# One mixer layer in float32: the down projection as Strassen's seven products, and another order of ScalarE's copies and norms

## The chip, the cores and the metric

The kernel runs on one core of one Trainium2 chip, as one launch. The metric is the device time of one execution in microseconds (us), the lower the better. A core has five instruction streams: TensorE (PE) multiplies matrices, VectorE (DVE) and ScalarE (ACT) work element by element, GpSimd (POOL) does small work and issues DMAs, SyncE (SP) issues DMAs only. They run side by side, each in its own order, and wait for each other by semaphores. Tiles live in SBUF (128 partitions), products are summed up in PSUM banks of 128x512 values, tensors named `..._d` lie in DRAM.

## The reference, cut to what matters

```python
def reference(x, c, ...):
    mod = silu(c) @ w_ada + b_ada
    sh1, sc1, g1, sh2, sc2, g2 = split(mod, 6)
    h = x * (1 + sc1) + sh1
    z = h @ w_in + b_in                        # seven slices of 256
    y = concat(short_conv(z), pool(z), conformer(z), ssm(z)) @ w_o
    x = layer_norm(ALPHA * x + (1 + g1) * y, ln1_g, ln1_b)
    h = x * (1 + sc2) + sh2
    f = (silu(h @ w_gate) * (h @ w_up)) @ w_down
    return layer_norm(ALPHA * x + (1 + g2) * f, ln2_g, ln2_b)
```

There are 1024 tokens, the model's width is 1024, the inner width of the last part (`D_FF`) is 2816 = 22 x 128, all in float32.

## The kernel before

Every float32 product is made of three matmuls of a short type: an operand is split into a high half (a cast on ACT, L80) and a low half (a subtraction on DVE, L81), and `passes` (L130 to L132) adds high x high, high x low and low x high into one PSUM bank. A pair of halves that waits for its matmuls is called a pair tile (`pr`); a wait on L80 or L81 is a wait for such a half.

The work comes in stages: input projection and mixers (0 to about 250 us), output projection and first layer norm of the first token half, gate and up projection with the mixers of the second half in between, the output projection and norm of the second half (about 390 to 515 us), then the rest of the gate and up projection by Strassen's scheme (515 to 785 us), then the down projection and the second norm. The code is written as generators. `in_order` keeps TensorE (and in places DVE and ACT) in the order in which the code is written; the other engines' instructions are put into order by a scheduler. `after(later, earlier)` orders two instructions of one engine without a wait.

**Mixers and output projection.** `out_prep(n, k)` makes the pair tile of 128 rows of `w_o` and the pair `ys` of one of the eight mixer outputs `y`; `out_step` multiplies them; `half(w3, c)` is the last slice of the input projection, which `short_out(1)` needs. `conformer(1)` ends with a norm: L457 scales on ACT, then transposes (L463) and a Silu (L464).

**Gate and up.** `c11(j)` makes the first two products of column block j for the first token half: after the first, `c11_mm` copies two banks on ACT (L643, "the copies of first products", tile `p1`), and only then TensorE goes on in the same banks. The norm of the second half (`ln1`, c = 1) is interleaved with it: its L580 scales a row tile on ACT, as soon as POOL has made the scale. `strassen(j)` makes the other five products of block j: inputs `a_ops(j)` (sums and differences of weight tiles, L725, and their pairs), products into banks `Z` and `X`, and after each product a DVE sum that reads the bank and lets TensorE go on (L757, L761, L767, L774, L778, two each). L769 and L781 multiply Silu(gate) by up, and POOL stores the products to `act_d` (L770, L782). The tiles `hi` come from a pool of three (`tmp`). `ada(j)` computes a column block of `mod` on DVE; `spread` writes a piece of `mod` to DRAM and reads it back as a row for all partitions (L470, tile `rowa_d`), and its last use, for g2, falls into Strassen's stage.

**Down.** For each token half c and each f of 22, `down_ops` loads `act_d` and `w_down`, makes both pairs, and `down_mm` multiplies them into eight banks (4 blocks t of 128 tokens, 2 halves h of the width): 2 x 22 x 4 x 2 x 3 = 1056 matmuls. `res2` and `ln2` then make the residual and the norm (L833, L834, statistics, a chain of small POOL steps for the inverse root, L841, L845), of the first token half beside the second's matmuls, and of the second as the tail.

## Time and profile before

| | |
|---|---|
| median of 3 executions | 1039.09 us (1038.07 to 1041.19) |
| the profiled execution, its time | 1037.87 us |
| its span, first to last instruction | 1036.1 us |
| TensorE busy | 980.8 us, 4480 matmuls |
| VectorE busy | 737.7 us |
| ScalarE busy | 344.5 us |
| GpSimd busy | 184.4 us |
| DMA | 177.75 MB, mean 172 GB/s |

Busy times are sums over the span of 1036.1 us; the time of an execution is 1.8 us longer than the span. The profile gives the granted clock of TensorE as a share of the full one, so 1.00 is 2.4 GHz and 0.50 is 1.2 GHz.

### The profile page before, as it was taken

To read this page: it belongs to the slowest core of one execution; us is meant where nothing else is said; L and a number is where in the kernel's file an instruction comes from. 1 tells how busy PE (TensorE), PEld (TensorE's weight loads), DVE (VectorE), ACT (ScalarE), POOL (GpSimd) and SP (SyncE) were. 2 spreads that over 40 slices of the span, in tenths; PEclk is the share of its full clock that TensorE was granted. 3 is DMA by queue.
4 is the path that set the end of the run, shared out by engine and by line. 5 is a ranking of instruction groups with operands and counts; after the bars stand their busy time and mean duration, and the time that the engine had idled before them with its cause. 6 is when DMAs were issued, how large, how long until landed. Compare 5 with 4: busy or idle time off the path is not lost.

```text
span 1036.1 us, 12527 instructions
## 1 busy us (share of the span) xinstructions
PE 980.8 (95%) x4480; PEld 799.9 (77%) x4480; DVE 737.7 (71%) x1184; ACT 344.5 (33%) x537; POOL 184.4 (18%) x515
## 2 busy tenths in 40 slices
...
GB/s 314 321 112 104 53 41 90 219 225 223 158 204 172 147 237 104 188 316 267 347 175 159 138 147 152 146 148 111 82 149 284 174 136 142 232 185 148 228 21 61
DMA packets 65694, 177.75 MB, mean 172 GB/s; under 512 B 11040, under 2 KB 17216, under 8 KB 65632
## 3 DMA queue, kind: packets, MB, share of 16 engines
...
## 4 chain that ended last, share of the span: by engine, by line
PE 60%; DVE 10%; DMA 5%; POOL 4%; ACT 3%; issue 2%; SPq 0%; DVEq 0%; POOLq 0%; ACTq 0%
PE mm L132 18%; PE mm L130 18%; PE mm L131 17%; PE sm L130 2%; PE sm L132 2%; PE sm L131 2%; DMA raw<-in_w_ada_dram 2%; DMA raw<-h_d 2%; DVE pr L81 1%; DVE acc L429 1%; DMA raw<-in_w_gate_dram 1%; DVE raw L168 1%; ACT tmp L598 1%; DVE lst L500 1%; POOL rs_a L397 1%
## 5 line engine op out<-in xcount | busy, mean ns | idle before, releaser
L81 DVE TENSOR_TENSOR pr<-raw,pr 128x1024 fp32r<-128x1024 f32 (+1 forms) x139 | 138.1, 1003 | 77.7 <-ACT pr L80 77.4
L80 ACT CAST pr<-raw 128x1024 fp32r<-128x1024 f32 (+1 forms) x139 | 119.2, 878 | 179.4 <-PE sm L132 68.4
L130 PE MATMUL mm<-bop,pr 128*128 128x512 f32 x264 | 103.2, 391 | 4.2 <-DVE c L767 3.5
L131 PE MATMUL mm<-bop,pr 128*128 128x512 f32 x264 | 102.8, 389 | 0.0
L132 PE MATMUL mm<-bop,pr 128*128 128x512 f32 x264 | 102.7, 389 | 0.0
L130 PE MATMUL mm<-h,pr 128*128 128x512 f32 (+1 forms) x208 | 77.0, 370 | 8.0 <-ACT p L643 7.1
L429 DVE SCALAR_TENSOR_TENSOR acc<-up,pack,acc 128x512 f32<-128x512 f32 x120 | 84.3, 742 | 0.1
L130 PE MATMUL mm<-pr,acts 128*128 128x512 f32 x216 | 84.0, 389 | 0.0
L131 PE MATMUL mm<-pr,acts 128*128 128x512 f32 x216 | 84.0, 389 | 0.0
L132 PE MATMUL mm<-pr,acts 128*128 128x512 f32 x216 | 84.0, 389 | 0.0
L132 PE MATMUL mm<-h,pr 128*128 128x512 f32 (+1 forms) x208 | 75.4, 362 | 2.9 <-DVE pr L81 2.9
L131 PE MATMUL mm<-h,pr 128*128 128x512 f32 (+1 forms) x208 | 75.2, 361 | 0.0
L132 PE MATMUL mm<-tb,pr 128*128 128x512 f32 x176 | 68.8, 391 | 1.1 <-DVE pr L81 1.0
L130 PE MATMUL mm<-tb,pr 128*128 128x512 f32 x176 | 68.7, 390 | 1.0 <-ACT pr L80 1.0
L131 PE MATMUL mm<-tb,pr 128*128 128x512 f32 x176 | 68.5, 389 | 0.0
L397 POOL TENSOR_SCALAR rs_a<-lmv 128x1 f32<-128x1 f32 x16 | 11.0, 689 | 318.1 <-DVE lmv L503 317.8
L168 DVE SCALAR_TENSOR_TENSOR raw<-raw,cond 128x1024 f32<-128x1024 f32 x48 | 58.1, 1218 | 13.3 <-DMA raw<-in_w_ada_dram 13.2
L80 ACT CAST pr<-room 128x512 fp32r<-128x512 f32 x60 | 34.3, 619 | 87.9 <-PE mm L132 83.9
L130 PEld LDWEIGHTS mm<-bop,pr 128*128 128x128 f32 x264 | 49.6, 188 | 16.4 <-DVE c L767 2.9
L132 PEld LDWEIGHTS mm<-bop,pr 128*128 128x128 f32 x264 | 49.6, 188 | 10.3
L131 PEld LDWEIGHTS mm<-bop,pr 128*128 128x128 f32 x264 | 49.6, 188 | 10.1
L131 PE MATMUL mm<-h_a,pr 128*128 128x512 f32 x104 | 42.7, 410 | 13.7 <-DVE h_a L81 13.5
...
## 6 DMA issues: line engine op xcount, KB each, us to landing
...
```

The lines of the kernel that those rows point to most:

```text
L80: S.copy(hi, src)
L81: V.tensor_tensor(out=lo, in0=src, in1=hi.bitcast(F32), op=SUB)
L130: PE.matmul(o, wh, xh, start=first, stop=False, skip_group_check=True)
L131: PE.matmul(o, wh, xl, start=False, stop=False, skip_group_check=True)
L132: PE.matmul(o, wl, xh, start=False, stop=last, skip_group_check=True)
L168: V.scalar_tensor_tensor(out=w, in0=w, scalar=1.0, in1=cond, op0=MUL, op1=MUL, accum_out=mod[:, j:j + 1])
L397: G.tensor_scalar(out=a, in0=v, scalar1=EPS, scalar2=None, op0=ADD)
L429: V.scalar_tensor_tensor(out=o, in0=u, scalar=dww[:, i, j:j + 1], in1=o, op0=MUL, op1=ADD)
L500: V.bn_stats(st[:, h], r[:, h * 512:(h + 1) * 512])
L598: S.activation(dst, src, AF.Identity, scale=hA[:, kk:kk + 1], bias=hB[:, kk:kk + 1])
```

## The change

The down projection is taken as a product of 2 x 2 blocks (token halves and inner halves on one side, inner halves and width halves on the other) and made of seven block products instead of eight, each over 11 blocks j: 7 x 11 x 4 x 3 = 924 matmuls. The sums of activations that five of the products need are made in `strassen(j)` as soon as the activations are there (L794 to L798, four of 128x512 on DVE) and stored to a new tensor `s_d` (two stores of 512 KB on POOL's queue, L797 and L799); for that the product of the first token half is read back from `act_d` (L777, 256 KB), and the store that stood in that place is gone. The product of the second token half's gate and up stays in SBUF until the sums are made. The differences of weights are made on DVE beside the products (`t13`, `t2`, `t34`). One product after another is summed up in four banks (`oA`) or the other four (`oB`); results that are wanted later are copied out by ACT. There are seven pair tiles where there were four, `GR` groups two j for one load, and in the last product the four last groups run t by t.

In Strassen's loop the inputs of block j + 1 (`a_ops`) are now begun ahead of the sums of block j. Before 515 us: both halves of `w3` are multiplied ahead of `out_prep`; `ada(32)` and `ada(33)` come later; the second part of `conformer(1)` is placed one c11 block later; the norm activations of `conformer(1)` and of `ln1` for c = 1 are ordered behind the latest copy of a first product; the order of `ln1` and `c11` around the output projection of the second half differs.

```diff
@@ -454,8 +454,10 @@
         G.tensor_scalar(out=nb, in0=nb, scalar1=-1.0, scalar2=None, op0=MUL)
         yield
         for t in range(4):
-            S.activation(nt[:, t * 256:(t + 1) * 256], tp[t // 2][:, (t % 2) * 256:(t % 2) * 256 + 256],
-                         AF.Identity, scale=rs[:, t:t + 1], bias=nb[:, t:t + 1])
+            i = S.activation(nt[:, t * 256:(t + 1) * 256], tp[t // 2][:, (t % 2) * 256:(t % 2) * 256 + 256],
+                             AF.Identity, scale=rs[:, t:t + 1], bias=nb[:, t:t + 1])
+            if c == 1 and t == 0:
+                after(i, copied[-1])
...
@@ -577,7 +580,9 @@
         nb = cst.tile([P, 1], F32, name="lnb", bufs=2)
         G.tensor_scalar(out=nb, in0=nm, scalar1=rs, scalar2=-1.0, op0=MUL, op1=MUL)
         yield
-        S.activation(r, r, AF.Identity, scale=rs, bias=nb)
+        i = S.activation(r, r, AF.Identity, scale=rs, bias=nb)
+        if c == 1:
+            after(i, copied[-1])
...
+    copied = []
+
     def c11_mm(w, z, p1, q, lo=0, n=CH):
 
         hs = slice(lo, lo + n)
         for i in range(2):
             product(z[i][:, hs], w[i], q, ("11", "21")[q], q == 0, q == 1, hs)
             if q == 0:
-                S.copy(p1[:, i * CH + lo:i * CH + lo + n], z[i][:, hs])
+                copied.append(S.copy(p1[:, i * CH + lo:i * CH + lo + n], z[i][:, hs]))
...
-    def strassen(j):
-
-
-        ao = a_ops(j)
-        w = next(ao)
+    def strassen(j, ao=None, w=None):
+
+
+        ao = ao or a_ops(j)
+        w = w or next(ao)
...
@@ -767,7 +774,7 @@
             V.tensor_tensor(out=c12[m], in0=c12[m], in1=X[m], op=ADD)
         S.activation(c12[0], c12[0], AF.Silu)
         V.tensor_tensor(out=c12[0], in0=c12[0], in1=c12[1], op=MUL)
-        G.dma_start(act_d[2 * j][:, CH:], c12[0])
+        G.dma_start(c12[1], act_d[2 * j][:, :CH])
...
-    def down_ops(c, n):
-        b0, b1 = FB[c][n]
-        w, act = {}, {}
-        more = sl.tile([P, 4, 2, 1024], F32R, name="wd", tag="ha") if b1 - b0 > 3 or c == 1 and n == 0 else None
-        if c == 1 and n == 0:
-            dn["first"] = more
-        for f in range(b0, b1):
-            a = raw_p.tile([P, 1024], F32, name="raw", tag="raw", bufs=4)
-            SP.dma_start(a[:, :CH], act_d[f][:, cs(c)])
-            act[f] = acts[(c * FT + f) % 8]
-            split(act[f][:, 0], act[f][:, 1], a[:, :CH])
-            if c == 1 and n < 4:
-                w[f] = dn["first"][:, n]
-            elif f < b1 - 3:
-                w[f] = more[:, f - b0]
-            else:
-                w[f] = pair_tile()
-            split(w[f][:, 0], w[f][:, 1], raw(A["w_down"][f]))
-        dn[c][n] = w, act
...
+        yield
+
+        a11, a21, (a12, a22) = c12[1], c12[0], [hi[0][:, H[c]] for c in range(2)]
+        (s1, s3), (s2, s4) = P1, [hi[1][:, H[c]] for c in range(2)]
+        V.tensor_tensor(out=s1, in0=a21, in1=a22, op=ADD)
+        V.tensor_tensor(out=s2, in0=s1, in1=a11, op=SUB)
+        V.tensor_tensor(out=s3, in0=a11, in1=a21, op=SUB)
+        G.dma_start(s_d[j, 0].rearrange("p a t -> p (a t)"), p1)
+        V.tensor_tensor(out=s4, in0=a12, in1=s2, op=SUB)
+        G.dma_start(s_d[j, 1].rearrange("p a t -> p (a t)"), hi[1])
+
+
+
+    GR = tuple((j, min(j + 2, FT // 2)) for j in range(0, FT // 2, 2))
...
+    def dn_pair(src, pt=None):
+        pt = pair_tile() if pt is None else pt
+        n = src.shape[1]
+        split(pt[:, 0, :n], pt[:, 1, :n], src)
+        return pt
+
+    def dn_mm(o, lt, rt, g, t, first, last):
+        n = GR[g][1] - GR[g][0]
+        for j in range(n):
+            ls, rs = slice(j * CH + t * P, j * CH + (t + 1) * P), slice(j * CH, (j + 1) * CH)
+            passes(o[t], (lt[:, 0, ls], lt[:, 1, ls]), (rt[:, 0, rs], rt[:, 1, rs]),
+                   first and g == 0 and j == 0, last and g == len(GR) - 1 and j == n - 1)
+
+    def dn_product(o, left, right, first, last, also=lambda g: None, room=(None, None)):
+        for g in range(len(GR)):
+            lt, rt = [dn_pair(x(g), None if g else y) for x, y in zip((left, right), room)]
+            for t in range(4):
+                dn_mm(o, lt, rt, g, t, first, last)
+            also(g)
...
@@ -884,11 +910,12 @@
         zz.append(half(w2, 1))
         short_out(0, zz)
         fin1()
+        zz = [half(w3, c) for c in (1, 0)][::-1]
         for n in range(2):
             wy.append(out_prep(n, K0[n]))
-            ada(32 + n)
         acc, taps = conv(1)
-        zz = [half(w3, c) for c in range(NCH)]
+        for j in range(32, 34):
+            ada(j)
         g1row = spread(mod[:, 16:24], "rowa")
         for j in range(34, 40):
             ada(j)
@@ -977,7 +1004,9 @@
                 run(taps)
                 conf = conformer(1, acc, sm)
                 with tc.high_priority():
-                    run(conf, 2)
+                    run(conf, 1)
+            if f == CF + 1:
+                run(conf, 1)
...
@@ -1004,11 +1033,13 @@
             cc.extend(c11(j) for j in range(GU_FIRST + 2, FT // 2))
             run(cc[0], 1)
         out_proj1(mid, done)
+        run(ln[0], 1)
         for t in range(4):
-            run(ln[t], 1)
             if t % 2 == 0:
                 run(cc[t // 2 + 1], 1)
             run(cc[t // 2], 1)
+            if t < 3:
+                run(ln[t + 1], 1)
             run(ln[t])
...
-        run(st)
+        run(st, 2)
         room = sl.tile([P, 8, 1024], F32, name="room", tag="ha")
         for j in range(1, FT // 2):
-            run(strassen(j))
+            ao = a_ops(j)
+            w = next(ao)
+            run(st)
+            st = strassen(j, ao, w)
+            run(st, 5)
             if j > 1 and j < 10:
                 ada(38 + j)
+        run(st)
...
+    pairs.extend((sl, f"m_{n}", 1) for n in ("up", "zch", "zp"))
     with in_order(ON_PE):
-        last = len(FB[0]) - 1
...
+        r0, r1 = [[yp.tile([P, 1024], F32, name="r2", tag=f"y{4 * c + t}") for t in range(4)] for c in range(2)]
+        oA = [mm() for _ in range(4)]
+        oB = [mm(), mm(), sm(), sm()]
...
+        def t13(g):
+            b12, b11, b22 = (w_rows(g, b, h, tmp()) for b, h in ((0, 1), (0, 0), (1, 1)))
+            V.tensor_tensor(out=kept(g), in0=b12, in1=b11, op=SUB)
+            V.tensor_tensor(out=kept(g, True), in0=b22, in1=b12, op=SUB)
+
+        def t2(g):
+            b22, o = w_rows(g, 1, 1), kept(g)
+            V.tensor_tensor(out=o, in0=b22, in1=o, op=SUB)
+            return o
+
+        def t34(g):
+            b21, o = w_rows(g, 1, 0), kept(g)
+            V.tensor_tensor(out=o, in0=b21, in1=o, op=SUB)
+            return kept(g, True)
+        dn_product(oA, lambda g: act_rows(g, 0, 0), lambda g: w_rows(g, 0, 0), True, False, t13)
         for t in range(4):
-            run(res2(o0, t, rr[t], x1[t]))
-        for n in range(len(FB[1])):
-            if n > 3:
-                down_ops(1, n)
...
+            S.copy(r0[t][:, H[0]], oA[t])
+        ln0, ln1_ = [[ln2(c, t, (r0, r1)[c][t]) for t in range(4)] for c in range(2)]
+        dn_product(oB, lambda g: sum_rows(g, 0, 0), kept, True, False)
+        x1 = [keep_x1(0, t, kx[:, t] if t < 3 else tmp()) for t in range(4)]
+        for t in range(4):
+            res2(r0[t], x1[t], 0, r0[t][:, H[0]])
+        dn_product(oA, lambda g: sum_rows(g, 1, 0), t2, False, False)
+        for t in range(4):
+            S.copy(r0[t][:, H[1]], oA[t])
+        dn_product(oA, lambda g: sum_rows(g, 0, 1), t34, False, False)
+        for t in range(4):
+            res2(r0[t], x1[t], 1, r0[t][:, H[1]])
+        x1 = [keep_x1(1, t, kx[:, t] if t < 3 else tmp()) for t in range(4)]
+        for t in range(4):
+            S.copy(r1[t][:, H[1]], oA[t])
+            V.tensor_tensor(out=r1[t][:, H[1]], in0=r1[t][:, H[1]], in1=oB[t], op=ADD)
+        dn_product(oA, lambda g: act_rows(g, 1, 1), kept, False, True)
+        for t in range(4):
+            res2(r1[t], x1[t], 1, r1[t][:, H[1]])
+            run(ln1_[t], 1)
+        for t in range(4):
+            res2(r1[t], x1[t], 0, oA[t])
+
+        more0 = sl.tile([P, 2, 2, 1024], F32R, name="wd0", tag="hb0")
+
+        def more_res(t, h, o):
+            f = sl.tile([P, CH], F32, name="f", tag=f"acc{t % 2}")
+            V.tensor_tensor(out=f, in0=o, in1=g2row[:, H[h]], op=MUL)
+            V.tensor_tensor(out=r0[t][:, H[h]], in0=r0[t][:, H[h]], in1=f, op=ADD)
+        dn_product(oA, lambda g: act_rows(g, 1, 0), lambda g: w_rows(g, 1, 0), True, True,
+                   room=[more0[:, i] for i in range(2)])
+        for t in range(2):
+            run(ln1_[t])
+        more = sl.tile([P, 4, 2, 1024], F32R, name="wd", tag="ha")
...
+        ops = []
+        for g in range(len(GR)):
+            two = (None, None) if g < len(GR) - 2 else [more[:, 2 * (g - len(GR)) + 4 + i] for i in range(2)]
+            ops.append((dn_pair(sum_rows(g, 1, 1), two[0]), dn_pair(w_rows(g, 1, 1), two[1])))
+            if g < last:
+                for t in range(4):
+                    dn_mm(oB, *ops[g], g, t, False, True)
+            if g in (1, 3):
+                run(ln1_[2 + g // 2])
+        for t in range(4):
+            more_res(t, 0, oA[t])
+            run(ln0[t], 1)
+        for t in range(4):
+            for g in range(last, len(GR)):
+                dn_mm(oB, *ops[g], g, t, False, True)
     with in_order(ON_DVE):
         for t in range(4):
-            run(ln[t], 2)
-            if t == 2:
-                run(ln[3], 1)
-            run(ln[t])
+            more_res(t, 1, oB[t])
+            run(ln0[t], 1)
+            if t:
+                run(ln0[t - 1])
+            run(ln0[t], 1)
+        run(ln0[3])
```

Three places show what the change moves. The first is ACT at about 233 us of the kernel before, in the first steps of the output projection. `ys` are the pairs of mixer outputs, `pr_2149` (before) and `pr_2150` (after) is the pair tile of the third `w_o` block. Before:

```order
L852 ACTIVATE y0_1164<-mm_1938,pack0_88 128x512
L381 ACTIVATE y3_1167<-mm_1968,pack2_471 128x512
L80 CAST pr_2149<-raw_2147 128x1024
L80 CAST ys_1976<-y4_1168 128x512
L80 CAST ys_1976<-y5_1169 128x512
L80 CAST ys_1976<-y2_1166 128x512
L80 CAST ys_1976<-y3_1167 128x512
L852 ACTIVATE y1_1165<-mm_2021,pack0_88 128x512
L80 CAST ys_1976<-y0_1164 128x512
```

After:

```order
L878 ACTIVATE y0_1164<-mm_1939,pack0_88 128x512
L381 ACTIVATE y3_1167<-mm_1969,pack2_471 128x512
L80 CAST ys_2027<-y4_1168 128x512
L80 CAST ys_2027<-y5_1169 128x512
L80 CAST ys_2027<-y2_1166 128x512
L80 CAST ys_2027<-y3_1167 128x512
L878 ACTIVATE y1_1165<-mm_1972,pack0_88 128x512
L80 CAST ys_2027<-y0_1164 128x512
L80 CAST pr_2150<-raw_2148 128x1024
```

The pair tile's cast stood ahead of the four `ys` casts and now comes behind all of them.

The second is ACT at about 429 us of the kernel before, in the norm of the second token half. `r1` is a row tile of that norm, `p1` the copy of a first product. Before:

```order
L580 ACTIVATE r1_3530<-r1_3530,lnb_3552,lrs_3536 128x1024
L80 CAST pr_3349<-raw_3670 128x1024
L80 CAST pr_3674<-raw_3675 128x1024
L580 ACTIVATE r1_3568<-r1_3568,lnb_3590,lrs_3574 128x1024
L643 COPY p1_3681<-mm_3679 128x512
L643 COPY p1_3681<-mm_3680 128x512
L598 ACTIVATE tmp_3718<-mm_3708,hB_1647,hA_1646 128x128 x4
```

After:

```order
L583 ACTIVATE r1_3531<-r1_3531,lnb_3553,lrs_3537 128x1024
L80 CAST pr_3350<-raw_3671 128x1024
L80 CAST pr_3675<-raw_3676 128x1024
L650 COPY p1_3682<-mm_3680 128x512
L650 COPY p1_3682<-mm_3681 128x512
L583 ACTIVATE r1_3569<-r1_3569,lnb_3591,lrs_3575 128x1024
L603 ACTIVATE tmp_3721<-mm_3711,hB_1647,hA_1646 128x128 x4
```

The two copies stood behind the second norm activation and now stand ahead of it.

The third is DVE at the boundary of two blocks in Strassen's loop (a middle one). `tmp_4915`, `tmp_4916` (before) and `tmp_4940`, `tmp_4941` (after) are the `hi` tiles of block j, the next two `tmp` those of block j + 1; `room_4331` and `room_4332` hold weights and first products. Before:

```order
L781 TENSOR_TENSOR tmp_4915<-tmp_4915,tmp_4916 128x1024
L81 TENSOR_TENSOR pr_5163<-room_4331,pr_5163 128x512
L757 TENSOR_TENSOR tmp_5102<-room_4331,mm_5104 128x512
L757 TENSOR_TENSOR tmp_5103<-room_4331,mm_5105 128x512
L81 TENSOR_TENSOR pr_5168<-room_4331,pr_5168 128x512 x2
L761 TENSOR_TENSOR c12_5100<-room_4331,mm_5104 128x512
```

After:

```order
L788 TENSOR_TENSOR tmp_4940<-tmp_4940,tmp_4941 128x1024
L796 TENSOR_TENSOR room_4332<-c12_4938 128x512
L794 TENSOR_TENSOR room_4332<-c12_4938,tmp_4940 128x512
L764 TENSOR_TENSOR tmp_5133<-room_4332,mm_5135 128x512
L795 TENSOR_TENSOR tmp_4941<-room_4332,c12_4938 128x512
L81 TENSOR_TENSOR pr_5194<-room_4332,pr_5194 128x512
L798 TENSOR_TENSOR tmp_4941<-tmp_4940,tmp_4941 128x512
L81 TENSOR_TENSOR pr_5199<-room_4332,pr_5199 128x512
L764 TENSOR_TENSOR tmp_5134<-room_4332,mm_5136 128x512
```

Between the product of the two activations (L781, now L788) and the second sum that frees a bank (the second L757, now L764) stood two instructions, and now seven do, four of them the new sums. In the pool of three, `tmp_5134` gets the buffer of `tmp_4940`, so the second L764 waits for the store of `tmp_4940` to `act_d`, which was not so before.

## Rows read from the trace of the kernel before

**Rows 1.** The page: busy us, share of the span, instructions, by engine.
```profile
PE 980.8 (95%) x4480; PEld 799.9 (77%) x4480; DVE 737.7 (71%) x1184; ACT 344.5 (33%) x537; POOL 184.4 (18%) x515
```
**Rows 2.** TensorE's waits: whom for, us in total, times, longest us.
```profile
PE mm L130 <- ACT p L643: 7.1, 2, 4.2
PE mm L132 <- DVE pr L81: 3.9, 4, 2.0
...
PE mm L130 <- ACT ys L80: 2.9, 1, 2.9
...
PE mm L132 <- DVE ys L81: 1.3, 1, 1.3
```
**Rows 3.** Stretches: us, busy by engine (instructions), granted clock, DMA share, GB/s.
```profile
237.70:244.50 6.80, 6.04 (x14) 4.79 (x15) 6.80 (x15) 1.35 (x3) 0.00 (x0) 0.50 0.67 232
...
432.20:439.10 6.90, 5.81 (x14) 4.56 (x15) 1.58 (x3) 5.22 (x14) 4.82 (x14) 0.51 0.53 210
...
515.00:785.00 270.00, 268.96 (x1186) 222.16 (x1185) 202.98 (x323) 75.66 (x121) 10.25 (x19) 1.00 0.42 147
...
785.10:1024.60 239.50, 239.50 (x1057) 198.05 (x1055) 141.25 (x171) 64.86 (x81) 27.26 (x64) 1.00 0.46 161
```
**Rows 4.** Timeline: start us, us, engine, instruction, [idle before, releaser]; loads and ACT, 231 to 238.
```profile
231.53 0.33 SPq L73 DMA_DIRECT2D raw<-in_w_o_dram  x1
...
234.83 1.04 ACT L80 CAST pr<-raw 128x1024 fp32r<-128x1024 f32 x1 [11.49 <-DMA raw<-in_w_o_dram]
235.78 2.17 ACT L80 CAST ys<-y 128x512 fp32r<-128x512 f32 x4
```
**Rows 5.** Timeline of ACT, 369 us.
```profile
369.34 1.93 ACT L457 ACTIVATE tmp<-sm,cnb,crs 128x256 f32<-128x256 f32 x4 [5.19 <-POOL cnb L454]
```
**Rows 6.** Timeline of ACT, 431 to 434 us.
```profile
431.53 1.24 ACT L580 ACTIVATE r<-r,lnb,lrs 128x1024 f32<-128x1024 f32 x1 [5.41 <-POOL lnb L578]
432.67 1.05 ACT L643 COPY p<-mm 128x512 f32<-128x512 f32 x2
```
**Rows 7.** Timeline of DVE and POOL at a boundary of two blocks, 620 to 629 us.
```profile
620.53 0.69 DVE L778 TENSOR_TENSOR tmp<-room,mm 128x512 f32<-128x512 f32 x1 [2.03 <-PE mm L132]
621.23 0.69 DVE L81 TENSOR_TENSOR pr<-room,pr 128x512 fp32r<-128x512 f32 x1
621.83 1.22 DVE L781 TENSOR_TENSOR tmp<-tmp 128x1024 f32<-128x1024 f32 x1
622.97 0.69 DVE L81 TENSOR_TENSOR pr<-room,pr 128x512 fp32r<-128x512 f32 x1
...
625.97 0.69 DVE L757 TENSOR_TENSOR tmp<-room,mm 128x512 f32<-128x512 f32 x1 [1.72 <-PE mm L132]
...
628.69 0.69 DVE L761 TENSOR_TENSOR c<-room,mm 128x512 f32<-128x512 f32 x1 [0.72 <-PE mm L132]
...
623.35 0.54 POOL L782 DMA_DIRECT2D act_d<-tmp  x1 [10.74 <-DVE tmp L781]
```
**Rows 8.** Landing of L782's stores and of L470's writes; timeline, 705 to 720 us.
```profile
DMA to landing us min/median/max: 2.9/2.9/8.6
...
L470 SPq DMA_DIRECT2D rowa_d<-mod x2: 377/378/378, 202.6 to 699.6; - x2
...
DMA to landing us min/median/max: 9.5/10.3/11.1
...
705.19 0.54 POOL L782 DMA_DIRECT2D act_d<-tmp  x1 [10.86 <-DVE tmp L781]
...
719.69 0.47 PE L130 MATMUL mm<-bop,pr 128*128 128x512 f32 x1 [1.04 <-DVE c L767]
```
**Rows 9.** Groups by line, 785 to 1025 us (busy us, mean ns); timeline of the tail.
```profile
L81 DVE TENSOR_TENSOR pr<-raw,pr 128x1024 fp32r<-128x1024 f32 x33 | 40.3, 1220 | 51.9 <-ACT pr L80 51.8
...
1025.17 0.68 DVE L833 TENSOR_TENSOR r<-sm,row 128x512 f32<-128x512 f32 x1
```

93 lines of the change are left out of this document (44 added, 49 removed).

## The prediction

> **What bounds the kernel now.** I read the page's engine shares first [rows 1]: TensorE (PE) is busy 95% of the span and VectorE (DVE) 71%, and the large stages run at the full clock [rows 3]. So TensorE is the bound, and there are two ways to gain: fewer matmuls, or fewer of the idle stretches that make up the other 5%. The waits of TensorE [rows 2] name what ends those stretches; the table of stretches [rows 3] tells which stages have none. The down stage, 785.1 to 1024.6 us, is one block: 1057 matmuls in 239.50 us, 0.2266 us each from start to start. Strassen's stage before it (515 to 785) is busy 268.96 of 270 us. The idle time therefore lies before 515 us, and in the 11.5 us between 1024.6 and the end. Two idle stretches are followed by stretches at a granted clock of about half, which is the 1.2 GHz level: 6.8 us after the wait at 233 to 236, and 6.9 us after the wait at 429 to 433. Each such stretch does half its length of full-speed work, so it costs about 3.4 us beyond the wait itself.
>
> **Down projection, matmuls.** Before: 2 token halves x 22 f x 4 t x 2 h x 3 passes = 1056. After: 7 products x 11 j x 4 t x 3 = 924. The 132 that go are of the shape whose pace is in [rows 3]: 132 x 0.2266 = 29.9 us less, if the stage stays without gaps. This is the one sure term.
>
> **Down projection, its operands.** Per group of two j (24 matmuls, 5.4 us) DVE makes the low halves of two 128x1024 pairs: at 1.22 us each [rows 9], 2.4 us. The weight differences add two such subtractions in the groups of product 1 and one in those of products 3 and 4, so product 1 needs 4.9 of each 5.4 us, if it is made at that pace; in the order its differences trail into product 2, which needs them later. With the residuals, the norms and the two rows scaled, I count 188 us of DVE work behind the last Strassen sum, against some 221 us of stage and tail; before it was 141 us in 239.5 [rows 3]. DVE becomes a close second. It is tightest in products 6 and 7: the instructions from the residual of product 5's result to the last pair come to 46 us, and the last pair is wanted about 45 us after that result. The copies of first products out of PSUM and the four-bank hand-overs between products add short chains of one ACT or DVE instruction (0.6 to 0.7 us each); the second bank set is free at most of them. Bounds: 0, if the pair tiles run ahead all the way, and 8 us, if every hand-over (six) shows a copy of 0.7 us and DVE is 4 us late at the end. I take 2 us.
>
> **Sums inside Strassen's loop.** Each of 11 rounds (27.2 us) gets four 128x512 DVE sums (0.60 us apiece start to start, 2.4 us) and two 512 KB stores, and loads 256 KB instead of storing it. DVE has room in the mean: 202.98 of 270 us busy [rows 3], plus 10 x 2.4. The place that matters is the boundary of two rounds, in the third piece of order. Let B be the end of a round's last product, 620.5 us in [rows 7], where L778 stops waiting for TensorE. Before, the second L757 began at 625.97 and ended its idle wait on TensorE: DVE was early. After, the product of the two activations is followed by seven 128x512 instructions before the second L764: 621.83 + 1.14 + 7 x 0.6 = 627.2 us, done at 627.9 (1.14 and 0.60 are the steps from one start to the next in these rows). TensorE overwrites that bank when its next product ends, and L761 began on that at 628.69; so about 0.6 us of margin is left. L764 also waits for something new: its tile is the one that the store of L789 reads. That store, like L782 before, is issued at 623.35 and lands 2.9 us later [rows 7, 8], at 626.3, in time too. The loads of the next round's gate and up tiles follow it and now share the DMA engines with two 512 KB stores. I bound the ten boundaries by 0 (margin holds) and 10 us (1 us each, about the margin again), and take 2 us.
>
> **One bad boundary.** At 699.6 us the spread of g2 (L470, writes of 4 KB in all to rowa_d) is issued; the two such spreads took 9.5 and 11.1 us to land [rows 8]. The store of L782 that is issued in that time, at 705.19, I take for the one that landed after 8.6 us, where the median of the eleven is 2.9. Before, only loads waited for it, and TensorE lost 1.04 us at 719.69. After, the second L764 of the next round waits for this store: 705.19 + 8.6 = 713.8, plus 0.7 for itself, while TensorE wants the bank at B + 8 = 710.3. That is a wait of about 4 us, perhaps followed by 3.4 us of clock as at 429 us, and the old 1.0 us goes. Bounds 0 and 7; I take +4 us. The Trainium skill, "DMA: Bandwidth & Descriptors", section "Queues, rings and completion order", says that a DMA's semaphore increment lands only after every earlier write of the same DMA engine, across its queues. By that rule the late landing comes again, and the term stays at +4; if it was chance, the term would be -1. The 8.6 us beside 2.9 agrees with the rule.
>
> **Order changes before 515 us.** At 234.83 us ScalarE (ACT) cast a w_o pair whose load had only been issued at 231.53, and the four ys casts behind it kept TensorE waiting 2.9 us, and their low halves on DVE another 1.3, with half clock behind [rows 2 to 4]. After, these casts come before that pair (first piece of order): 4.2 us of waits and 3.4 of clock go. Next late are the w_o pairs of the following steps, made at DVE's and the loads' pace; I give back 1.6 and take -6 us, bounds -3 and -7.6. At 369 us the copies of a first product (L643) stood behind four norm activations that had waited 5.19 us for POOL [rows 5]: 2.9 of the 7.1 us in [rows 2], which go; the activations are the later part of a norm whose transposes follow only in the output projection. I take -3, bounds -3 and 0. At 431.53 us the same copies stood behind a norm activation (L580) that waited for POOL [rows 6]: 4.2 us of wait and 3.4 of clock. After, the copies come first (second piece). The norms, the tb pairs and the stores behind them start no earlier than before while TensorE arrives 7 us sooner, so part may come back up to 515: I take -6, bounds -2 and -7.6. At 288 us one w_up pair was 2.0 us late on DVE [rows 2]; it moves ahead in DVE's order. I take -1, bounds -2 and 0.
>
> **Tail.** The last four groups run t by t, 21 matmuls = 4.76 us per t, where DVE needs about 5.1 us per t; before there were 42. The chain after the last matmul is the same length: residual 0.7 us, 0.7 us, statistics, the POOL chain, two scalings and the store, 1025.17 to the end [rows 9]. I take +0.7, bounds 0 and 3.
>
> **Sum** against the profiled execution of 1037.87 us (span 1036.1): -29.9 + 2 (operands) + 2 (boundaries) + 4 (spread) - 6 (233 us) - 3 (368 us) - 6 (429 us) - 1 (288 us) + 0.7 (tail) = -37.2, so 1000.7. The median of the executions timed is 1.2 us above the profiled one, which gives **1002 us**.
>
> **Rivals.** *The early gaps only move.* The 16 us of gains before 515 us are worth nothing if the next pair, load or norm is late by the same: DVE is busy all of the 6.80 us around 240 [rows 3], which speaks for it; that the casts and copies had their data and stood only behind others' waits speaks against it. Keeping a fifth, 3 us: 1002 + 13 = 1015 us. *Nothing is lost late.* The margins hold, the down stage is gapless and the spread is absorbed: without the +8.7 and with the early gains at 18 instead of 16: 1002 - 11 = 991 us. Against it: the margins are under 1 us. *Every boundary becomes a DMA wait.* The store that L764 waits for lands late not once but in every round, since two more 512 KB stores and the prefetched gate and up loads of the next round lie around it. At the 8.6 us of [rows 8] a boundary costs 4 us and then 3.4 of half clock, 7.4 us; ten instead of one cost 67 us more: 1069 us, slower than before. It decides from six boundaries: the 37 us of the sum are eaten by five more than the one counted. For it: the landing time under load is shown once. Against it: the other stores of this kind have a median of 2.9 us, and the DMA engines are busy 42% in this stage, at 147 GB/s [rows 3]. *The change does not do what it says*: 924 matmuls stand in the order, so only the ScalarE part could fail, which is the first rival.
>
> **How the numbers follow.** Forecast (995 to 1009) 0.58; early gaps only move 0.20; nothing lost late 0.16; every boundary 0.04; something between, near no change, 0.02. The range from 990 to 1016 holds the forecast, the middle of its two neighbours, and leaves out under 2 in 10. A measurement of this kernel tells 0.3% (3 us) from no change. Faster by more: 0.95; within: 0.02; slower: 0.03.
>
> **What would show it.** In the changed profile: 924 matmuls in the last stage at 0.227 us, so about 210 us of it, and its waits on DVE pairs under 8 us; no wait on ACT ys near 233 and on p near 368 and 429, and no stretch at half clock behind them; one wait of TensorE of about 4 us near 690, behind an L764 that waits for a DMA; L764's waits elsewhere below 1 us; the tail about 12 us. The forecast is wrong if DVE is busy over 95% in products 6 and 7 with TensorE waiting for pairs, or if L764 waits in every round.

## The result, and the profile after

The changed kernel takes 1025.18 us (median of 4 runs, 1023.93 to 1026.33), beside 1040.09 us for the kernel before on the same chip (1038.07 to 1041.19): a ratio of 0.986, 95% interval 0.9836 to 0.9884. It is faster by 15 us (1.4%), but the forecast was 1002 us and the range ended at 1016. The profiled execution took 1024.31 us with a span of 1022.5, 13.6 us less than the span of before.

The page of after, busy us by engine, answers to [rows 1]; under it the stretches of after (us, busy by engine with instructions, granted clock, DMA share, GB/s), which answer to [rows 3]:

```profile
PE 960.3 (94%) x4348; PEld 779.2 (76%) x4348; DVE 807.9 (79%) x1268; ACT 358.0 (35%) x545; POOL 200.1 (20%) x537
```

```profile
0.00:225.00 225.00, 203.71 (x972) 158.68 (x973) 176.83 (x360) 74.18 (x114) 79.07 (x281) 0.95 0.51 160
225.00:515.00 290.00, 272.37 (x1267) 224.50 (x1266) 209.25 (x323) 129.98 (x222) 64.91 (x141) 0.96 0.62 214
515.00:791.70 276.70, 272.69 (x1189) 223.44 (x1189) 225.21 (x361) 75.25 (x119) 21.47 (x40) 0.99 0.54 186
791.70:1008.20 216.50, 211.49 (x925) 172.58 (x923) 187.99 (x216) 78.60 (x91) 26.43 (x58) 1.00 0.65 217
```

The 132 matmuls are gone (4480 to 4348). But the last line begins at 791.7 us, where the down stage of before began at 785.1: the kernel reaches that stage 6.5 us later, not 10 us earlier as the sum had it. And the mean clock of 225 to 515 us is lower than before. The same stretch of the kernel before:

```profile
225.00:515.00 290.00, 268.08 (x1266) 220.89 (x1265) 209.22 (x320) 129.70 (x222) 65.05 (x142) 0.98 0.60 215
```

TensorE's waits in after (whom for, us in total, times, longest), to be set beside [rows 2]:

```profile
PE mm L130 <- ACT p L650: 5.6, 2, 2.9
PE mm L131 <- DVE pr L81: 4.7, 5, 2.2
PE mm L132 <- DVE pr L81: 3.6, 4, 2.0
PE mm L130 <- DVE y L877: 3.2, 1, 3.2
PE mm L130 <- DVE tmp L764: 2.9, 2, 2.2
...
PE sm L130 <- ACT y L466: 2.0, 1, 2.0
```

The wait on ACT `ys` has fallen from 2.9 to 0.3 us; a wait on `y` from L877 stands there that was not, the one on L466 has grown from 0.5 to 2.0 us, and the copies of first products still cost 5.6 us where they cost 7.1.

Here is where the time went, measured on TensorE from the first matmul of each stage (profiled executions, us; "again" is a second profile of the changed kernel, from another session, "undone" is the kernel with all early order changes taken back, from the same session as "again"; the last three are kernels of the experiments, "best" the one with two edits):

| stage | before | after | after, again | undone | after, fewer loads | undone, fewer loads | best |
|---|---|---|---|---|---|---|---|
| start to first output step | 236.4 | 234.2 | 234.6 | 239.3 | 234.7 | 238.2 | 232.7 |
| to the second half's output projection | 140.9 | 141.2 | 141.4 | 140.5 | 139.3 | 140.5 | 137.0 |
| to Strassen's block 0 | 88.6 | 94.8 | 95.0 | 88.4 | 93.0 | 88.4 | 86.7 |
| blocks 0 and 1 | 72.7 | 73.8 | 74.7 | 77.4 | 68.3 | 68.4 | 78.5 |
| blocks 2 to 10 | 246.3 | 247.4 | 252.0 | 252.4 | 249.6 | 251.1 | 250.9 |
| down stage | 239.5 | 216.5 | 219.2 | 219.5 | 217.5 | 220.2 | 218.9 |
| tail | 11.5 | 14.5 | 14.5 | 14.4 | 14.5 | 14.5 | 14.5 |

Each column is one execution; "again" shows the slowest of its six (1033.12 us, median 1028.71). How far executions of one early order differ is shown by four kernels further down (the stores on POOL's queue, the spread moved, the reuse in product 1, three groups at the end), which have the same instructions in the same order as after up to 512 us on TensorE, VectorE, ScalarE and GpSimd. With the two of after that makes six profiles: they reach the first output step at 234.2 to 235.9 us, take 91.2 to 95.0 us in the third row, and begin block 2 (the first four rows together) at 541.3 to 545.9 us. The two profiles with the early order undone and full loads begin it at 545.4 and 545.7 us.

### The profile page after: what moved, and what is told of

The parts are those of the page before. It is cut to its first block, busy times and chain, and to the rows that moved or that the text cites. A ratio compares the mean times of both kernels' runs of the same rounds, so it can differ in the third digit from the quotient of the medians.

```text
span 1022.5 us, 12397 instructions
## 1 busy us (share of the span) xinstructions
PE 960.3 (94%) x4348; PEld 779.2 (76%) x4348; DVE 807.9 (79%) x1268; ACT 358.0 (35%) x545; POOL 200.1 (20%) x537
## 4 chain that ended last, share of the span: by engine, by line
PE 29%; issue 26%; DVE 11%; POOL 8%; DMA 7%; ACT 3%; SPq 0%; POOLq 0%; DVEq 0%; ACTq 0%
PE mm L132 9%; PE mm L130 9%; PE mm L131 9%; DVE pr L81 3%; DMA tmp<-in_w_down_dram 2%; DVE acc L429 1%; DMA raw<-in_w_ada_dram 1%; DVE raw L168 1%; POOL rs_b L402 1%; ACT tmp L603 1%; POOL rs_a L397 1%; DMA raw<-h_d 1%; ACT pr L80 1%; PE sm L130 1%; DMA raw<-in_w_o_dram 1%
## 5 line engine op out<-in xcount | busy, mean ns | idle before, releaser
L80 ACT CAST pr<-raw 128x1024 fp32r<-128x1024 f32 (+1 forms) x157 | 133.6, 876 | 178.5 <-PE mm L132 67.8
L81 DVE TENSOR_TENSOR pr<-raw,pr 128x1024 fp32r<-128x1024 f32 (+1 forms) x157 | 155.3, 1002 | 32.9 <-ACT pr L80 32.4
L131 PE MATMUL mm<-pr 128*128 128x512 f32 x250 | 97.9, 391 | 4.7 <-DVE pr L81 4.7
L130 PE MATMUL mm<-pr 128*128 128x512 f32 x250 | 97.4, 390 | 0.1
L132 PE MATMUL mm<-pr 128*128 128x512 f32 x250 | 97.3, 389 | 0.0
L429 DVE SCALAR_TENSOR_TENSOR acc<-up,pack,acc 128x512 f32<-128x512 f32 x120 | 84.6, 749 | 0.1
L130 PE MATMUL mm<-h,pr 128*128 128x512 f32 (+1 forms) x208 | 78.2, 376 | 6.5 <-ACT p L650 5.6
L132 PE MATMUL mm<-h,pr 128*128 128x512 f32 (+1 forms) x208 | 76.4, 367 | 2.9 <-DVE pr L81 2.9
L131 PE MATMUL mm<-h,pr 128*128 128x512 f32 (+1 forms) x208 | 76.6, 368 | 0.0
L130 PE MATMUL mm<-tb,pr 128*128 128x512 f32 x176 | 69.5, 395 | 2.9 <-DVE tmp L764 2.9
L132 PE MATMUL mm<-tb,pr 128*128 128x512 f32 x176 | 69.6, 396 | 0.7 <-DVE pr L81 0.7
L131 PE MATMUL mm<-tb,pr 128*128 128x512 f32 x176 | 69.0, 392 | 0.0
L131 PEld LDWEIGHTS mm<-pr 128*128 128x128 f32 x250 | 46.9, 188 | 16.2 <-DVE pr L81 6.7
```

Source lines behind the costliest of these rows:

```text
L80: S.copy(hi, src)
L81: V.tensor_tensor(out=lo, in0=src, in1=hi.bitcast(F32), op=SUB)
L130: PE.matmul(o, wh, xh, start=first, stop=False, skip_group_check=True)
L131: PE.matmul(o, wh, xl, start=False, stop=False, skip_group_check=True)
L132: PE.matmul(o, wl, xh, start=False, stop=last, skip_group_check=True)
L429: V.scalar_tensor_tensor(out=o, in0=u, scalar=dww[:, i, j:j + 1], in1=o, op0=MUL, op1=ADD)
```

## Where the early gains went

**At 238 us.** The `ys` come in time, and TensorE then stops 4 us later. DVE in after, 237 to 242 us, and TensorE (start us, us, engine, instruction, [idle before, releaser]):

```profile
238.08 1.21 DVE L168 SCALAR_TENSOR_TENSOR raw<-raw,cond 128x1024 f32<-128x1024 f32 x1
...
239.30 0.74 DVE L429 SCALAR_TENSOR_TENSOR acc<-up,pack,acc 128x512 f32<-128x512 f32 x1
...
240.69 0.74 DVE L877 SCALAR_TENSOR_TENSOR y<-mm,pack,y 128x512 f32<-128x512 f32 x1
```
```profile
237.90 0.39 PE L132 MATMUL mm<-pr,ys 128*128 128x512 f32 x1
241.49 0.50 PE L130 MATMUL mm<-pr,ys 128*128 128x512 f32 x1 [3.20 <-DVE y L877]
```

L877 reads the PSUM bank of one `w3` half. That half is now multiplied ahead of the output steps, so its bank is held until DVE, which has `ada` and the convolution (L429) in front, comes to it. The change took away a wait on casts and put a bank that is given back late in its place: 3.2 us for 4.2.

**At 446 and 463 us.** ACT in after, the copies of first products (L650), and TensorE behind them:

```profile
440.20 2.94 ACT L603 ACTIVATE tmp<-mm,hB,hA 128x128 f32<-128x128 f32 x8
...
444.07 2.08 ACT L80 CAST pr<-raw 128x1024 fp32r<-128x1024 f32 x2
445.96 1.16 ACT L650 COPY p<-mm 128x512 f32<-128x512 f32 x2
...
458.52 2.90 ACT L603 ACTIVATE tmp<-mm,hB,hA 128x128 f32<-128x128 f32 x8
...
462.39 1.12 ACT L650 COPY p<-mm 128x512 f32<-128x512 f32 x2
```
```profile
446.68 0.76 PE L130 MATMUL mm<-h,pr 128*128 128x512 f32 x1 [2.88 <-ACT p L650]
...
463.07 0.50 PE L130 MATMUL mm<-h,pr 128*128 128x512 f32 x1 [2.72 <-ACT p L650]
```

Compare [rows 6]: the norm activation is no longer ahead of the copies, and the 5.41 us wait for POOL is not in their way. But the next thing in ACT's order is: eight L603 of the norm (2.9 us) and casts. One wait of 4.2 us became two of 2.9 and 2.7.

**The clock.** Five waits that are new in after (on `y`, on L466 at 387.5 us, two on the copies, and one on L764 at 520.6 us) are each followed by a stretch at half clock. So are two waits that stood in before as well, near 289 and 316 us, where before has none. Stretches of after (columns as above):

```profile
242.00:245.40 3.40, 3.40 (x9) 2.65 (x9) 3.40 (x7) 0.00 (x0) 0.00 (x0) 0.50 0.63 231
388.70:392.10 3.40, 3.40 (x10) 2.63 (x9) 2.17 (x3) 1.58 (x3) 0.00 (x0) 0.50 0.02 5
446.80:450.20 3.40, 3.40 (x8) 2.67 (x9) 0.79 (x1) 3.40 (x9) 2.16 (x4) 0.50 0.92 342
463.80:467.20 3.40, 3.40 (x10) 2.65 (x9) 3.31 (x6) 0.00 (x0) 0.56 (x1) 0.50 0.99 388
521.80:525.20 3.40, 3.40 (x10) 2.66 (x9) 1.87 (x4) 0.00 (x0) 0.00 (x0) 0.51 0.73 293
289.70:293.10 3.40, 3.40 (x18) 3.40 (x18) 1.41 (x3) 2.93 (x5) 2.31 (x7) 0.51 0.92 370
317.00:320.40 3.40, 3.40 (x10) 2.66 (x9) 3.40 (x6) 0.00 (x0) 0.00 (x0) 0.51 0.97 364
```

Seven stretches of 3.4 us at about 1.2 GHz, 23.8 us together, cost about 11.9 us of full-speed work. Before there were two between 225 and 525 us [rows 3], 6.8 and 6.9 us, which cost 6.9. So the clock alone takes 5 us. The waits did get shorter in sum before 515 us: of the 290 us from 225 on TensorE is idle 17.6 us in after and 21.9 in before (the two rows above), 4.3 us less. But six of the seven stretches lie there; they cost 10.2 us of work against 6.9, which takes back 3.3 of the 4.3. Over the whole span TensorE is idle 62.2 us in after and 55.3 in before, more by the waits in Strassen's stage and the down stage and by the tail.

## Experiments

### The early order changes, one by one

The first kernel undoes all order changes before 515 us, so that only the down projection as seven products and the sums for it are left; the other three undo one each. The three edits (lines with - are of after):

```diff
-            if c == 1 and t == 0:              # the conformer's norm
-                after(i, copied[-1])
...
-                    run(conf, 1)
-            if f == CF + 1:
-                run(conf, 1)
+                    run(conf, 2)
```
```diff
-        if c == 1:                             # ln1
-            after(i, copied[-1])
...
-        run(ln[0], 1)
         for t in range(4):
+            run(ln[t], 1)
...
-            if t < 3:
-                run(ln[t + 1], 1)
```
```diff
-        zz = [half(w3, c) for c in (1, 0)][::-1]     # w3
         for n in range(2):
             wy.append(out_prep(n, K0[n]))
+            ada(32 + n)
         acc, taps = conv(1)
-        for j in range(32, 34):
-            ada(j)
+        zz = [half(w3, c) for c in range(NCH)]
```

> All order edits ahead of 515 us undone (w3, ada, conformer, norms, c11 around the norm); the seven products, the sums in Strassen's loop and the tail stay. Theory A (the early edits only moved the waits: the last gate/up column of the second half starts its tb products 4.3 us later than before, the rest gains 18): about 1020 us, with the first tb product back at 466 us. Theory B (the early edits gained what the prediction gave them, 16 us, and the loss lies in Strassen's loop and the down stage): about 1041 us.

> The changed kernel with the norm of the second half as before: L583 not ordered behind the copies, ln and c11 in the old order. Theory A: the waits at 443 and 460 us go and the 4.3 us wait at 429 with its 6.9 us at half clock comes back; net 1 to 3 us faster, 1022 to 1024. Theory B: 6 us slower, 1031.

> The changed kernel with the conformer's second part where it was and L457 not ordered behind a copy. Theory A: the 2.9 us wait at 368 us comes back, the 2.2 us wait at 385 us (with 3.4 us at half clock) goes: 0 to 2 us faster, 1023 to 1025. Theory B: 3 us slower, 1028.

> The changed kernel with the w3 halves and ada 32 and 33 where they were. Theory A: the first output steps start at 236.4 us instead of 234.2 with 6.8 us at half clock instead of 3.4, and without the 3.4 us wait at 238: 1 to 2 us slower, 1026 to 1027. Theory B: 6 us slower, 1031.

Measured on one chip, beside 1044.0 us of before: all undone 1032.46 us (ratio 0.989, 0.9861 to 0.9918); norm undone 1029.73 (0.9873, 0.9829 to 0.9916); conformer undone 1031.34 (0.9878, 0.9844 to 0.9912); `w3` undone 1030.21 (0.986, 0.9823 to 0.9896). The changed kernel had 0.986 in its own session. So the early changes together are worth some 0.3%, about 3 us, with intervals that overlap, and no single one can be told from nothing. They are not shown to be a net loss, and they are far from a gain of 16: neither reading holds as it was put. The kernel with all of them undone says a second thing: the seven products with their sums, the boundaries, the spread and the tail are worth 11.5 us here, where the terms of the sum for them come to 21.2 (29.9 less the 8.7 of costs).

### What takes the gain near 440 to 515 us

The copies of first products move from ACT to DVE for the blocks beside the norm, so that nothing of the norm on ACT stands in front of them:

```diff
-                copied.append(S.copy(p1[:, i * CH + lo:i * CH + lo + n], z[i][:, hs]))
+                dst = p1[:, i * CH + lo:i * CH + lo + n]
+                copied.append(S.copy(dst, z[i][:, hs]) if not late else V.tensor_copy(dst, z[i][:, hs]))
...
-        c11_mm(w, z, p1, 0)
+        c11_mm(w, z, p1, 0, late=j > GU_FIRST)
```

> The changed kernel with the copies of first products behind the second half's norm (three columns, two 128x512 copies each) on VectorE instead of ScalarE. Theory A (ScalarE's queue of norm work holds the copies up: the two waits of 2.9 us at 443 and 460 us): both waits go, the first tb product starts 5 to 9 us earlier (about 462 to 465 us), the kernel is 4 to 9 us faster. Theory B (the copies wait for data that comes late anyway, so moving them only shows the next wait, on the norm's loads): the tb product starts within 2 us of 470.

1026.86 us, 0.9851 (0.9827 to 0.9875). The last stretch before block 0 gets shorter, 45.6 to 41.2 us (44.0 to 45.6 in the six profiles of the changed early order): the waits on the copies are four of at most 1.6 us, 4.3 in all. Block 0 gets longer, 41.0 to 46.2 (41.0 to 45.3 in the six): part is given back, in a place where the DMA engines are busy 93% at 332 GB/s. I took that for the cause and cut the loads there: the second-factor operands of three products (tile `bop`) loaded to a quarter, the rest zero-filled by POOL, so this kernel leaves out part of the computation.

```diff
         def load(t, src):
-            SP.dma_start(t, src)
+            SP.dma_start(t[:, :128], src[:, :128])
+            G.memset(t[:, 128:], 0.0)
             return t
```

> The kernel with the copies on VectorE, and the 24 loads from h2 and t1, t2 for the t operands cut to a quarter (128 of 512 columns; POOL fills the rest with zeros, so the t operands are wrong for three token quarters of that half): 4.6 MB less to move around 470 to 500 us. Theory A (what gave back the 4.4 us of the copies is the load of the DMA engines, 0.93 busy at 332 GB/s from 480 to 515 us): from the first tb product to the second block's takes 40 to 43 us instead of 46, and from the second half's first c11 product to the second block 4 to 7 us less. Theory B (ScalarE's and VectorE's splits set that pace): within 1.5 us of the kernel with the copies on VectorE.

1017.11 us, 0.9733 (0.9703 to 0.9763): block 0 falls from 46.2 back to 40.8 us. That fits the DMA engines taking back what the order won. But it does not show it: the loads could cost the same in any order. So the same cut was made in the changed kernel and in the one with the early order undone, beside both of them with full loads, all on one chip.

> The changed kernel, in which the operands of the three weight-difference sets (the tiles bop of the fourth stage's end) are loaded only to a quarter and the rest is zero-filled by POOL, so the output is not the reference's; copies stay on ACT. It takes 24 loads down to a quarter, all between about 430 and 515 us. Theory A (the early order changes are worth their 16 us, but the DMA engines, full at 430 to 515 us, take them back): faster than the changed kernel by 8 to 12 us, and more than the same edit gains in the kernel with the early order undone. Theory B (the early waits only move from one place to the next, whatever the DMA does): faster by the same 3 to 8 us that the same edit gains there.

> The same quarter loads, but with all order changes before 515 us undone, so only Strassen's down projection is left of the change; output not the reference's. Theory A: the wait on ACT p behind the norm activations (4.2 us and half clock, near 430 us in the kernel before) is no DMA wait and stays; so this kernel gains at most 4 us on the kernel with the early order undone and full loads, and the gap to the changed kernel with quarter loads is 8 us or more. Theory B: the gap between the two kernels with quarter loads is the same 0 to 5 us as between the two with full loads.

> The changed kernel again, beside the others on the same chip, so that the differences are between runs of one chip. Both theories: 0.983 to 0.989 of the kernel before.

> The changed kernel with all order changes before 515 us undone, again, on the same chip as the changed kernel. From the earlier ratios (0.989 and 0.986): slower than the changed kernel by 3 us, 0 to 6.

| | full loads | quarter loads |
|---|---|---|
| early order as changed | 1028.71 us, 0.9859 (0.9828 to 0.989) | 1020.05 us, 0.9771 (0.9741 to 0.9802) |
| early order undone | 1033.8 us, 0.9881 (0.9844 to 0.9917) | 1020.32 us, 0.9786 (0.9756 to 0.9816) |

By the medians the order changes are worth 5 us with full loads, which the intervals do not tell from nothing, and 0.3 us with the loads cut. If the DMA engines were what takes the 16 us back, the gap would have grown to 8 us or more; it did not, so that explanation falls. The loads are a cost of their own, 9 to 13 us, in either order: with them cut both kernels begin block 2 at about 535 us, with full loads both at 545.7. The stretch 480 to 515 us shows how, in after again, undone, and the two with quarter loads, in this order:

```profile
480.00:515.00 35.00, 31.06 (x129) 24.94 (x128) 26.76 (x44) 13.82 (x23) 3.31 (x7) 0.95 0.88 314
```
```profile
480.00:515.00 35.00, 31.93 (x137) 25.18 (x136) 28.35 (x47) 15.51 (x27) 3.78 (x7) 1.00 0.91 328
```
```profile
480.00:515.00 35.00, 34.05 (x150) 27.55 (x148) 31.05 (x50) 15.05 (x26) 8.78 (x21) 1.00 0.83 289
```
```profile
480.00:515.00 35.00, 34.50 (x153) 28.26 (x152) 32.02 (x52) 16.09 (x28) 9.87 (x23) 1.00 0.80 284
```

With full loads TensorE is idle 3 to 4 of 35 us there whatever the order (DMA share 0.88 to 0.91), with quarter loads under 1. Up to 470 us the waits are those of the full loads: with the order as changed 3.2 us at 238 and 2.9 + 2.8 us at L650, with it undone 3.9 us on `ys` and 4.2 + 2.9 at the copies. Most of the early gains therefore move from one wait to the next, on ACT, DVE and PSUM banks, and the table by stage says the same: the second row is level, the third is 6.6 us worse than undone (2.8 to 6.6 over the six profiles), the first 4.7 better (3.4 to 5.1), blocks 0 and 1 2.7 better.

### Does the gain last where the new wait is removed too?

The two `w3` halves get banks of the other PSUM pool, so that L877 holds no bank that the output steps want; one kernel has this alone, one has it with the DVE copies above.

```diff
-    def half(w, c):
-        o = mm()
+    def half(w, c, bank=mm):
+        o = bank()
...
-        zz = [half(w3, c) for c in (1, 0)][::-1]
+        zz = [half(w3, c, sm) for c in (1, 0)][::-1]
```

> The changed kernel with the two w3 halves in the two sm banks instead of two of the six mm banks. Theory A (the 3.4 us wait at 238 us is for a PSUM bank that L877 on VectorE gives back late, behind taps and ada): the wait goes, and the 3.4 us at half clock with it, first c11 product 3 to 5 us earlier, 281 instead of 285. Theory B (the output steps are paced by the w_o pairs and VectorE anyway): the wait moves to the third w_o pair near 241 to 243 us, gain under 1.5 us.

> Only the w3 halves in banks of the other pool, again, beside the former on one chip. If the 3 us of stage time saved behind 238 us last: 0.983 of the kernel before. If they are taken back later: 0.986, the ratio of the changed kernel.

> Two edits together: both w3 halves in banks of the other pool, and the late copies of first products on DVE in place of ACT. If the waits near 238 us and near 446 to 463 us are causes of their own, their gains add: 0.980 of the kernel before (0.983 for the first alone, 0.985 for the second alone, 0.986 for the changed kernel). If a gain is always taken back by the next wait before 515 us: 0.983 to 0.986.

Alone: 1023.8 us, 0.9828 (0.9784 to 0.9871), and on another chip 1026.64 us, 0.984 (0.9812 to 0.9867). With the DVE copies: 1023.35 us, 0.9815 (0.9789 to 0.9842). TensorE in the kernel with both, 236 to 250 us, has neither the wait nor the half clock:

```profile
236.00:250.00 14.00, 14.00 (x63) 11.36 (x61) 13.26 (x26) 2.35 (x4) 0.00 (x0) 1.00 0.74 238
```

From the first output step to the first `c11` block TensorE takes 47.6 to 48.6 us in the three, 50.9 in after. Block 2 begins at 533.9, 539.7 and 534.9 us in the three, beside 541.3 to 545.9 in the six profiles with the banks of after. So the stage time that is won lasts up to there, though some comes back (blocks 0 and 1 take 78.5 us in the kernel with both, 73.8 in after). The whole times do not settle it: the intervals hold the readings for a gain that lasts and for one that is taken back, and whether the two gains add is not shown. The kernel with both is the fastest kernel that computes everything: 0.9815 beside 0.986 and 0.9859 for the changed one. The intervals still touch, so a gain of 4 us over the changed kernel is likely and not certain.

### The boundary with the spread of g2

The write of the g2 row is taken out of SP's order in Strassen's stage and issued late, on POOL's queue, behind everything POOL has to do up to then.

```diff
-    g2row = spread(mod[:, 40:48], "rowa")
+    with tc.issue_after(last_g):
+        g2row = spread(mod[:, 40:48], "rowa", G)
```

> The changed kernel with the spread of g2 issued on POOL's queue behind the last store of the sums, after Strassen's loop. Theory A (the spread's slow landing holds the store that the second L764 waits for): the boundary of the eighth and ninth block costs 27.2 us in this and every profile, where it costs up to 33 with the spread there; 0 to 5 us faster. Theory B (the late landing is of the stores and loads themselves): a boundary of 30 us or more stays.

1032.5 us, 0.9899 (0.9854 to 0.9944). The block's round takes 27.2 us, the plain length, where the eighteen profiles that kept the place show 28.2 to 34.1 (the middle of them 32.6). The landing of the stores that DVE's second L764 waits for, in after, in after again and with the spread moved, in this order:

```profile
DMA to landing us min/median/max: 2.8/2.9/5.1
```
```profile
DMA to landing us min/median/max: 2.8/2.9/7.7
```
```profile
DMA to landing us min/median/max: 2.9/2.9/3.9
```

And who waits for them: DVE in after, then in after again, with TensorE behind the latter and its clock from 721 us:

```profile
717.16 0.69 DVE L764 TENSOR_TENSOR tmp<-room,mm 128x512 f32<-128x512 f32 x1 [1.13 <-DMA act_d<-tmp]
```
```profile
720.43 0.69 DVE L764 TENSOR_TENSOR tmp<-room,mm 128x512 f32<-128x512 f32 x1 [3.77 <-DMA act_d<-tmp]
...
721.27 0.77 PE L130 MATMUL mm<-tb,pr 128*128 128x512 f32 x1 [3.32 <-DVE tmp L764]
```
```profile
721.30:724.70 3.40, 3.40 (x8) 2.73 (x9) 2.16 (x4) 0.00 (x0) 0.00 (x0) 0.50 0.97 346
```

So the predicted wait is there, with its cause, at 718 and 721 us; its size changes from execution to execution, 0.7 us in the first profile and 3.3 in the second, and only the second has half clock behind it. The Trainium skill, "DMA: Bandwidth & Descriptors", section "Queues, rings and completion order", has a semaphore's increment land only behind the earlier writes of the same DMA engine; a store's maximum of 3.9 us without the small writes and 5.1 to 8.6 with them agrees with it. Moving the spread gains nothing, though: issued at 797.9 us among the full DMA engines of the down stage it takes 14.8 us to land, and TensorE then waits 5.6 us:

```profile
818.21 0.80 PE L131 MATMUL mm<-pr 128*128 128x512 f32 x1 [5.62 <-DVE pr L81]
```

### The down stage and the tail

Four kernels try the waits that are left after 791 us. First, the stores of the output of the second token half go to POOL's queue, so that SP's loads do not stand behind them.

```diff
-SP.dma_start(out[tok * P:(tok + 1) * P, hs], r[:, hs])
+(G if c else SP).dma_start(out[tok * P:(tok + 1) * P, hs], r[:, hs])
```

> The changed kernel with the stores of the second half's result (L872, c = 1) on POOL's queue instead of SyncE's. Theory A (the 2.3 us wait at 974 us comes from w_down and s_d loads behind stores that wait for the norm on SyncE's queue): that wait falls below 0.5 us and the down stage gets 2 to 4 us shorter. Theory B (VectorE's L871 waits for POOL with the pairs behind it): the wait stays above 1.5 us.

1029.08 us, 0.9885 (0.9853 to 0.9917). In after DVE waits 2.73 us for POOL's chain at 974 us, the pairs stand behind it, and TensorE waits 2.15 us:

```profile
974.21 0.75 DVE L871 SCALAR_TENSOR_TENSOR r<-r,lrs,row 128x512 f32<-128x512 f32 x1 [2.73 <-POOL lrs L415]
974.88 2.35 DVE L81 TENSOR_TENSOR pr<-raw,pr 128x1024 fp32r<-128x1024 f32 x2
...
976.15 0.50 PE L131 MATMUL mm<-pr 128*128 128x512 f32 x1 [2.15 <-DVE pr L81]
```

With the stores moved, there are four waits of 0.6, 0.7, 1.3 and 1.0 us between 973 and 990 instead: 3.5 us where there were 3.1.

Second, the differences of weights in product 1 take a quarter of `w_down` from the tile that the product has loaded itself, in place of a second load.

```diff
-            b12, b11, b22 = (w_rows(g, b, h, tmp()) for b, h in ((0, 1), (0, 0), (1, 1)))
+            b12, b22 = (w_rows(g, b, 1, tmp()) for b in range(2))
+            b11 = first_w[g]
```

> The changed kernel with two loads instead of three per group for the weight differences: the third is the block that product 1 has loaded already. Theory A (products 1 and 2 are held up by the loads: the DMA engines are busy 0.88 to 0.91 of that time): the waits of TensorE there (0.5, 0.7 and 0.9 us) fall below 0.5 us in all, DMA share under 0.85, the down stage 1 to 3 us shorter (214 to 216 us). Theory B (VectorE's amount of work holds them up, 28.7 of 30.5 us in product 2): no change.

> The changed kernel with the w3 halves in the sm banks and two loads per group for the weight differences. If both gains hold beside each other: 4 to 6 us faster than the changed kernel, ratio to before about 0.981. If they are only moved: 0.985.

1037.66 us, 0.9917 (0.9889 to 0.9945), a loss of 6 us: the tile is held until DVE has made the difference (it ends at 815.90 us), the next load of `w_down` is issued behind that, at 815.92, and TensorE waits 5.38 us for ACT's cast at 822 us. The DMA share in product 1 falls from 0.91 to 0.82, and it is slower all the same; neither reading had that. With the other banks for `w3` as well it is 1029.33 us, 0.9843 (0.9809 to 0.9877): the loss here beside the gain there (down stage 224.5 us).

Third, only three groups in place of four run t by t at the end.

```diff
-        last = len(GR) - 4
+        last = len(GR) - 3
```

> The changed kernel with three groups run t by t in the last product instead of four: 15 matmuls, 3.4 us per t, not 21, 4.8 us. Theory A (the end is set by VectorE's 5.3 us per t, begun when the first t is summed up): the first sum comes 4.1 us later against the last, so the time from the last matmul to the end grows from 14.5 to 18 to 19 us. Theory B (the end is a fixed chain after the last matmul): it stays at 14.5.

1032.39 us, 0.9873 (0.9833 to 0.9912), with a tail of 16.4 us for 14.5. That lies between the two readings (18 to 19, and 14.5): fewer matmuls beside the chain leave more of it behind the last matmul, so DVE's step bears on the end, but only half of the growth that was expected from it came. DVE in the tail of after, and TensorE's last matmul:

```profile
1008.01 1.41 DVE L871 SCALAR_TENSOR_TENSOR r<-r,lrs,row 128x512 f32<-128x512 f32 x2 [0.39 <-POOL lrs L415]
...
1010.54 0.68 DVE L1132 TENSOR_TENSOR f<-sm,row 128x512 f32<-128x512 f32 x1
...
1013.30 1.42 DVE L871 SCALAR_TENSOR_TENSOR r<-r,lrs,row 128x512 f32<-128x512 f32 x2 [0.39 <-POOL lrs L415]
...
1018.07 1.42 DVE L871 SCALAR_TENSOR_TENSOR r<-r,lrs,row 128x512 f32<-128x512 f32 x2 [2.16 <-POOL lrs L415]
```
```profile
1007.63 0.39 PE L132 MATMUL sm<-wd 128*128 128x512 f32 x1
```

From one L871 to the next DVE takes 5.29 us, TensorE's 21 matmuls 4.76. The last residual (L1132) starts at 1010.54, 2.5 us behind the end of the last matmul; before it started 0.6 us behind it [rows 9].

## Why the prediction was wrong

The sum said -37.2 us and the profiled time fell by 13.6; the miss is 23.6 us. By its terms, from the two profiles (the first two rows part at the start of block 1 in Strassen's stage, 509.8 us in before and 511.3 in after):

| term | predicted | measured | miss |
|---|---|---|---|
| order changes before 515 us (233, 368, 429, 288) | -16 | +1.5 | 17.5 |
| Strassen's boundaries and the spread | +6 | +4.9 | -1.1 |
| matmuls and operands of the down stage | -27.9 | -23.0 | 4.9 |
| tail | +0.7 | +3.0 | 2.3 |

Two single executions stand behind this table, and the runs with the order undone share out the miss differently. By them the early changes, forecast at -16, are worth 3 to 5 us. The rest of the change, forecast at -21.2, is worth 11.5 and 9.6 us beside before in the same session. So 11 to 13 us of the miss lie in the order changes and 10 to 12 behind them. Beside the profile of before, the two undone profiles show that second part as 8 us in the down stage over the sum, some 3.5 between block 1 and the down stage, and 2 in the tail; as before was not profiled in those sessions, this split is not certain.

**Order changes before 515 us: the step that failed.** Each wait named was read rightly, and all but the one at 288 us are gone or smaller. What was wrong is that I priced them as waits that end, where each is one in a row. At 233 us I gave back 1.6 of 7.6 us; the bank held by L877 took 3.2 us, and 1.7 us more in 3.4 us at half clock. I had looked at what the casts wait for, and not at who holds the banks once `w3` goes first. At 429 us I gave back 1.6 of 7.6; two waits of 2.9 and 2.7 us with half clock behind both took all of it. I had looked for the activation that waited for POOL, and not at the eight L603 and the casts that come next in ACT's order before the copies. At 368 us the 2.9 us became 2.05 us at 387.5, behind L466, the end of the conformer's norm that the change places later, with half clock behind it. At 288 us the wait stayed at 2.04 us, and a slow stretch came behind it. In time, by the runs with the order undone, the early changes are worth 3 to 5 us (0.3 with the loads cut), not 16. That is the rival "the early gaps only move", which kept a fifth, 3 us; for it spoke the line that DVE is busy all of the 6.80 us around 240 [rows 3], and I gave it 0.20. Its own figure, 1015 us, is 10 us short too, as it kept the other terms of the sum.

**The clock.** I took a wait's cost as the wait plus half of the slow stretch that followed, and a removed wait as both saved. That a new wait of 2 to 3 us brings a slow stretch of its own was not counted; these bring 5 us more than before.

**Down stage.** The matmul term holds: 924 x 0.2266 = 209.4 us is what 216.5 us contain. The operands were to cost 2 us (0 to 8) and cost 7.1, in the second profile 9.8. Of the 7.1 us 4.7 are five waits on `pr`: three in product 2, where DVE is busy 28.2 of 30 us and the DMA engines 88%, one of 2.15 us and one of 0.94 us around the start of product 7. The sign given for this term did not come: DVE is busy 82, 77 and 92% of the stretches 942 to 972, 972 to 988 and 988 to 1008 us, not over 95. The term was mis-sized, within its own bounds or 2 us beyond them.

**Strassen's boundaries and the spread: the sum right, in the first profile by luck.** +4.9 for +6 in the first profile, +6.9 in the second, 5 to 10 us over the fifteen profiles with full loads and the spread in its place. In the first profile the parts miss in opposite directions: the boundaries cost 5.3 us for +2, and the round with the spread takes 28.2 us, 0.3 less than before, for +4. In the second they are 1.7 and 5.2. The four sums in front of L764 do cost something, but mostly at the first boundary (2.2 us at 520 us, the round 3.8 us longer), where DVE also makes the weights' pairs; the later ones keep their margin but for 1.4 us over six rounds. In the three kernels with the loads cut that first round is at most 0.8 us longer than before, so its cost hangs on the loads as well. The spread costs what was forecast, in most executions: the middle of its rounds is 32.6 us beside 28.5 before.

**Tail.** I saw that DVE needs 5.1 us for each t and TensorE 4.76, and took it as if that difference came once. DVE's step measured 5.29 us with POOL's 0.39 us in each, and the lag adds up over the four t: 1.9 of the 3.0 us are the later start of the last residual. The rest stands behind it, and no run here takes it apart. The measured 3.0 us is the upper bound given.

**The other rivals.** "Nothing is lost late" and "every boundary becomes a DMA wait" are both out: the stores' median landing stayed at 2.9 us with two more stores each round.

**What stays open.** The kernels with the early order of before reach the first output step at 238.2 to 239.5 us, the kernel before at 236.4, with the same order of instructions there. In their sessions the kernel before was also 3 to 4 us slower in its median; whether that explains it was not tried, and before has one profile. So the 3 to 5 us for the early changes rest on medians with intervals of about 3 us on each side.
